# The recurrent mixer of a three-mixer network: its projections, its local part and its solve put in another order

## The chip, the cores and the metric

One core of one Trainium2 chip runs the whole program. The metric is device time in microseconds (us) of one execution; the kernel before took 1224.47 us, the median of three runs between 1223.39 and 1226.15. The engines are PE (TensorE, matrix products and their weight loads), DVE (VectorE), ACT (ScalarE), POOL (GpSimd) and SP (SyncE, which here only issues transfers). DRAM is the chip's large memory, SBUF the memory of the engines, PSUM the banks that PE writes.

## The reference

512 tokens of width 1024 pass two blocks (neighbourhood attention, then grouped attention, each followed by a gated projection) and then a hybrid layer, which is what this change is about. Cut to that layer:

```python
h = rms_norm_2(x, norm_g); proj = h @ w_in
(q, kc, vc, ks, vs, kw, vw, gl, g_nsa, rwkv_in, g_rwkv) = _split(proj, IN_SIZES)
o_nsa = nsa_mixer(...) * silu(g_nsa)             # compressed, selected and windowed attention
# the recurrent mixer, 8 heads of 64
prev = pad(p)[:, :-1]; p = p + shift_mu * (prev - p)          # p is rwkv_in
r, k, v, wd, ad = _split(p, (512, 512, 512, 64, 64))
w = w0 + tanh(wd) @ w_up; decay = exp(-exp(-softplus(-w) - 0.5)); a = sigmoid(a0 + ad @ a_up)
kk = normalised(k * k_k); k = k * (1 + (a - 1) * k_a)
for t:                                                         # per head
    state = state * w_t + (state @ -kk_t) (kk_t * a_t)^T + v_t k_t^T
    y_t = state @ r_t
y = group_norm(y) * gn_w + gn_b + sum(r * k * r_k) * v
return x + concat(o_nsa, y * silu(g_rwkv)) @ w_out
```

## The kernel before, in words

Weights come as a stream of 512 KB pieces: SP loads a piece (`wraw`), ACT rounds it to `whi` (L147) and DVE or POOL takes the difference `wlo` (L148; `N.lo` says which of the two). Each product is three matmuls, high with high, high with low and low with high. Activations are kept the same way, as `act` and `half` tiles.

The 512 tokens are four tiles of 128. The first two blocks hold them in a swapped order (token 64 r + c of an 8 x 64 grid stands at 8 c + r); the hybrid layer needs them in their natural order. A store to DRAM can put them back row by row, and `natural` (L330) copies the whole activation into natural order in SBUF.

The recurrent mixer turns the loop over tokens into chunks:

- **Projections.** `rwkv_proj` makes r, k and v for four heads (`hh` is 0 or 1), 96 matmuls of 256 columns for each. PE's result is copied by ACT (L796), multiplied by `shift_mu` on DVE (L797), subtracted on POOL (L798), and both pieces go to DRAM (`d_raw`), one of them a row later, so that a load brings a token and its predecessor. `rwkv_lowrank` makes decay and learning rate (`d_low`), with eight small float32 products (L769).
- **Local part.** `rwkv_local` runs eight times (two groups of heads, four token tiles). Each loads its `rkv` rows (L841) and `low` rows (L837), adds the two pieces (L844), normalises k (L853 to L857), forms decayed sums on PE (L865), transposes (L890), splits into high and low (`l_xl`, `l_tl`, L222), multiplies (L920), masks (`am`, `abq`, L925 and L926) and stores triangles (`d_a`) and other pieces. The pool has four `rkv` and two `low` buffers, so two of the eight are under way at a time.
- **Solve.** `rwkv_triangles` loads all triangles at once, 128 blocks of 32 x 32 (L951). `rwkv_solve` inverts them in 31 steps on DVE (L967, L969) and stores the inverses (`d_t`, L972), whose other entries were zeroed before (L736).
- **Chain.** `rwkv_applied` loads an inverse (L995) and multiplies (L1003, the first PE work that needs the solve), and the rest follows token tile by token tile.

Between these steps `products()` feeds PE with the sparse attention's keys and queries and with the gates of the recurrent mixer (`rwkv_gates`, four weight pieces). The code order is only a wish: a scheduler at build time interleaves what the code emits, and from then on each engine runs its own list strictly in order. SP's list and ACT's list hold the transfers too, so a transfer that waits holds up what stands behind it.

Of the kernel before, what the change touches and what calls it, by code (L numbers as in the profile page):

```python
# [123 lines left out]
class Net:  # L124
# [197 lines left out]
    def natural(self, act):  # L322

        out = self.new_act()
        nc = self.nc
        engines = iter(TT * (nc.vector.tensor_copy, nc.vector.tensor_copy, nc.scalar.copy, nc.scalar.copy))
        for t in range(TT):
            for a, o in zip(act, out):
                for ks in (slice(0, 4), slice(4, 8)):
                    next(engines)(o[:, ks].rearrange("p k (r c) -> p k r c", r=8)[:, :, :, 16 * t:16 * t + 16],  # L330
                                               a[:, ks, t * P:t * P + P].rearrange("p k (c r) -> p k r c", r=8))
        return out
# [391 lines left out]
    def rwkv_consts(self, pool):  # L724
# [7 lines left out]
        zero = pool.tile([P, 768], F32, name="rkv", bufs=4)  # L732
        nc.vector.memset(zero, 0.0)
        for t in range(TT):
            for h in range(2):
                nc.sync.dma_start(out=self.head_rows(self.d_t, t, 4 * h, 4), in_=zero[:, :512].rearrange("p (h n) -> p h n", h=4))  # L736
# [10 lines left out]
    def rwkv_lowrank(self, buf, act):  # L747

        nc = self.nc
        ps = self.cols(("r_wa",), act)  # L750
        raw, d = buf[:, 0], buf[:, 1]
        nc.scalar.copy(raw.rearrange("p (r t c) -> p t c r", r=8, t=TT), ps.rearrange("p (t c r) -> p t c r", t=TT, r=8))
# [3 lines left out]
        nc.vector.tensor_sub(d[:, 1:], raw[:, :S - 1], raw[:, 1:])  # L756
        nc.vector.tensor_scalar(d[:, 0:1], raw[:, 0:1], -1.0, None, op0=OP.mult)
        nc.vector.scalar_tensor_tensor(d, d, mu, raw, op0=OP.mult, op1=OP.add)

        for j, (up, row) in enumerate((("decay_up", "decay_w0"), ("iclr_up", "iclr_a0"))):  # L760
            l, m = buf[:, 2 + 2 * j], buf[:, 3 + 2 * j]
            nc.scalar.activation(l[0:64], d[64 * j:64 * j + 64], AF.Tanh if j == 0 else AF.Copy)
            nc.vector.memset(l[64:65], 1.0)
            nc.sync.dma_start(out=m[0:64], in_=self.a[up])
            nc.sync.dma_start(out=m[64:65], in_=bass.AP(tensor=self.a[row].tensor, offset=self.a[row].offset,
                                                        ap=[[S, 1], [1, S]]))
            for t in range(TT):
# [15 lines left out]
    def rwkv_proj(self, act, hh, names, mu, stage):  # L783

        nc = self.nc
        for name in names:
            n = "rkv".index(name)
            keys = [("r_" + name, hh, j) for j in range(2)]
            self.fetch(*keys)
            us = [self.w.pop(k) for k in keys]  # L790
            for tp in range(2):
                ps = self.group_rows(us, act, tp)
                r = stage(n, tp)
                p2 = ps.rearrange("p (t n) -> p t n", t=2)
                m = mu[:, names.index(name), None, :].to_broadcast([P, 2, 256])
                nc.scalar.copy(r[0], p2)  # L796
                nc.vector.tensor_tensor(r[1], p2, m, op=OP.mult)  # L797
                nc.gpsimd.tensor_tensor(r[0], r[0], r[1], op=OP.subtract)  # L798
                for t in range(2 * hh):
                    for d, a in zip(self.d_raw[hh], r):  # L800
                        o = bass.AP(tensor=d.tensor, offset=d.offset + (1 + 16 * (2 * tp + t)) * 768 + 256 * n, ap=[[768, 16], [64 * 768, 8], [1, 256]])
                        nc.sync.dma_start(out=o, in_=a[:, t])

    def rwkv_proj_first(self, act, mu):

        raw = [self.act_tile(self.act, j, F32).rearrange("p k n -> p (k n)") for j in range(2)]
        full = [a[:, :TT * 768].rearrange("p (t n) -> p t n", t=TT) for a in raw]
        self.rwkv_proj(act, 0, "rkv", mu, lambda n, tp: [a[:, 2 * tp:2 * tp + 2, 256 * n:256 * n + 256] for a in full])
        for t in range(TT):
            for d, a in zip(self.d_raw[0], full):  # L810
                o = bass.AP(tensor=d.tensor, offset=d.offset + (1 + 16 * t) * 768, ap=[[768, 16], [64 * 768, 8], [1, 768]])
                self.nc.sync.dma_start(out=o, in_=a[:, t])
        return [a[:, TT * 768:].rearrange("p (a t n) -> p a t n", a=2, t=2) for a in raw]

    def rwkv_params(self, pool, hh):
        par = {n: self.bcast(pool, n, 256 * hh, 256) for n in ("k_k", "k_a", "r_k")}
        return par
# [139 lines left out]
    def rwkv_solve(self, pool, A, T):  # L957

        nc = self.nc
        for s in range(31):  # L960
            for j0, j1 in ((0, min(s + 1, 8)), (8, s + 1)):
# [7 lines left out]
                nc.vector.tensor_tensor(tv, tv, o, op=OP.subtract)  # L969
        for t in range(TT):  # L970
# [767 lines left out]
```

## Time and profile before

| what | value |
|---|---|
| median of three runs | 1224.47 us |
| the profiled execution | 1225.36 us, span 1223.6 us, mean granted clock 0.969 |
| busy over the span | PE 1138.2 us (93%), DVE 851.1 (70%), ACT 623.0 (51%), POOL 395.8 (32%) |
| chain that ended last | PE 61%, DVE 17%, DMA 7%, ACT 5%, issue 5%, POOL 3% |
| projections, low rank and copies (721 to 793 us) | PE busy 64.24 of 72 us, clock 0.93 |
| seven of the eight locals (824 to 924 us) | PE busy 90.15, DVE 86.60 of 100 us, clock 0.91 |
| solve | 942.11 to 980.88 us; first matmul of the chain at 990.22 us |

The span runs from the first to the last instruction; the execution's own time is 1.8 us longer. A busy PE is not a PE at its peak: its matmuls overlap, so a stretch is judged by the time from one start to the next, by the waits and by the granted clock, which is 1 at 2.4 GHz and 0.5 at 1.2 GHz. Times on DVE, ACT and POOL can be added up, save for some 0.07 us by which neighbours overlap.

### The profile page before, as it was taken

How to read it: one execution, taken by the hardware profiler on the slowest of the kernel's cores; microseconds unless marked ns; L12 is line 12 of the kernel's file. 1: busy time of each engine (PE TensorE's matmuls, PEld its weight loads, DVE VectorE, ACT ScalarE, POOL GpSimd, SP SyncE). 2: the span in 40 equal slices, each digit the busy share in tenths (PEclk: the TensorE clock that was granted, in tenths of full speed). 3: DMA queues.
4: the chain of work that ended last, by engine and by line, in shares of the span. 5: the costliest groups of instructions: out<-in, count | busy, mean ns of one | idle time of the engine just before them, and what ended most of it. 6: DMA issues, size and time to landing. Idle time of an engine off the chain costs nothing.

```text
span 1223.6 us, 20514 instructions
## 1 busy us (share of the span) xinstructions
PE 1138.2 (93%) x7176; PEld 999.8 (82%) x7176; DVE 851.1 (70%) x2093; ACT 623.0 (51%) x1355; POOL 395.8 (32%) x549
## 2 busy tenths in 40 slices
PE   7999999998999989999999999799899799899896
PEld 5898989886889868877877898688789688798785
DVE  6566666657677877886676763489786925688865
ACT  5566565635443566566564642434444223267743
POOL 0021211110300364674311011164445523357731
PEclk9999999999999989999999999899799989899998
DMA  6333333213232310211132445774667553712511
GB/s 248 117 98 102 102 103 102 92 61 132 93 108 74 97 38 1 70 35 36 52 130 69 139 120 192 219 262 145 202 189 195 162 140 106 237 45 71 180 52 69
DMA packets 87040, 143.24 MB, mean 117 GB/s; under 512 B 21525, under 2 KB 52245, under 8 KB 86938
## 3 DMA queue, kind: packets, MB, share of 16 engines
q1 hardware_dynamic: 72344, 133.49, 34.3%
q10 hardware_dynamic: 14018, 6.36, 2.0%
q0 software_dynamic: 576, 2.10, 0.5%
q8 instruction: 56, 0.92, 0.3%
q14 instruction: 46, 0.38, 0.1%
HBM read 114.12 MB, written 27.79 MB: 116 GB/s over the span
## 4 chain that ended last, share of the span: by engine, by line
PE 61%; DVE 17%; DMA 7%; ACT 5%; issue 5%; POOL 3%; SPq 2%; ACTq 0%; POOLq 0%; DVEq 0%
PE mm L205 23%; PE mm L188 5%; PE mm L189 5%; PE mm L190 4%; PE sc L205 3%; PE mm L216 2%; DVE KT L967 2%; PE tr L492 1%; PE u L677 1%; PE tr L670 1%; DMA rkv<-d_raw 1%; PE ch L1003 1%; DVE big L969 1%; PE u L1373 1%; PE tr L318 1%
## 5 line engine op out<-in xcount | busy, mean ns | idle before, releaser
L205 PE MATMUL mm<-whi,act 128*128 128x256 f32 (+2 forms) x1344 | 356.2, 323 | 9.7 <-DVE x L347 3.5
L205 PE MATMUL mm<-wlo,act 128*128 128x256 f32 (+2 forms) x896 | 287.1, 321 | 0.5 <-POOL wlo L148 0.5
L205 PEld LDWEIGHTS mm<-whi,act 128*128 128x128 f32 x1344 | 239.8, 194 | 31.3 <-DVE x L347 5.5
L205 PEld LDWEIGHTS mm<-wlo,act 128*128 128x128 f32 x896 | 174.7, 195 | 10.3 <-POOL wlo L148 0.7
L147 ACT CAST whi<-wraw 128x1024 fp32r<-128x1024 f32 (+1 forms) x128 | 133.3, 1043 | 91.9 <-PE mm L205 38.5
L148 DVE TENSOR_TENSOR wlo<-wraw,whi 128x1024 fp32r<-128x1024 f32 x91 | 116.6, 1284 | 54.2 <-ACT whi L147 52.4
L205 PE MATMUL mm<-whi,half 128*128 128x256 f32 (+1 forms) x448 | 146.0, 327 | 4.2 <-DVE half L222 4.2
L148 POOL TENSOR_TENSOR wlo<-wraw,whi 128x1024 fp32r<-128x1024 f32 (+2 forms) x37 | 88.0, 2382 | 129.7 <-DVE rs_y L237 69.9
L188 PE MATMUL mm<-act,whi 128*128 128x512 f32 x312 | 126.1, 404 | 2.2 <-DVE b_qn L547 2.2
L190 PE MATMUL mm<-act,wlo 128*128 128x512 f32 x312 | 124.6, 399 | 0.0
L205 PEld LDWEIGHTS mm<-whi,half 128*128 128x128 f32 x448 | 88.4, 198 | 10.8 <-DVE half L222 5.1
L484 POOL TENSOR_SCALAR a_P<-a_P,a_rd 128x256 f32<-128x256 f32 x64 | 32.9, 517 | 156.5 <-DVE a_rd L483 143.9
L189 PE MATMUL mm<-half,whi 128*128 128x512 f32 x200 | 79.1, 396 | 0.0
L188 PEld LDWEIGHTS mm<-act,whi 128*128 128x128 f32 x312 | 59.9, 192 | 14.4 <-issue 3.4
L190 PEld LDWEIGHTS mm<-act,wlo 128*128 128x128 f32 x312 | 59.9, 192 | 12.2
L663 POOL TENSOR_SCALAR b_P<-b_P,b_rd 128x512 f32<-128x512 f32 x64 | 45.5, 715 | 54.6 <-DVE b_rd L662 44.0
L660 ACT ACTIVATE b_P<-sc,b_mn 128x512 f32<-128x512 f32 x64 | 44.1, 690 | 21.5 <-DVE b_mn L657 13.6
L657 DVE TENSOR_REDUCE b_mn<-sc 128x1 f32<-128x512 f32 x64 | 43.5, 684 | 10.6 <-PE sc L655 10.2
L478 DVE CUSTOM_DVE_ANT_0 a_P<-sc,a_bias 128x256 f32<-128x256 f32 x64 | 26.1, 421 | 34.7 <-PE tr L492 20.1
L1359 POOL TENSOR_SCALAR n_P<-n_P,b_rd,n_gl 128x128 f32<-128x128 f32 (+3 forms) x64 | 39.2, 619 | 30.6 <-DVE b_rd L1357 10.3
L222 DVE TENSOR_TENSOR b_pl<-tr,b_ph 128x512 fp32r<-128x512 f32 x64 | 43.3, 683 | 6.0 <-ACT b_ph L221 5.3
L189 PE MATMUL mm<-act,whi 128*128 128x512 f32 x112 | 45.8, 409 | 0.0
(396 smaller groups left out, 2826.8 us busy)
## 6 DMA issues: line engine op xcount, KB each, us to landing
wraw<-in_wstream SPq DMA_DIRECT2D x133, 512.0 KB, 3.6
a_bias<-in_bias SPq DMA_DIRECT2D x16, 384.0 KB, 3.1
rkv<-d_raw SPq DMA_DIRECT2D x16, 384.0 KB, 4.9
d_raw<-act SPq DMA_DIRECT2D x8, 384.0 KB, 5.6
xf<-x SPq DMA_DIRECT2D x4, 512.0 KB, 3.7
d_low<-low ACTq DMA_DIRECT2D x8, 256.0 KB, 2.8
d_t<-rkv SPq DMA_DIRECT2D x8, 256.0 KB, 4.2
low<-d_low SPq DMA_DIRECT2D x8, 256.0 KB, 3.3
```

The source lines that it names most:

```text
L147: nc.scalar.copy(hi[:, :m], raw[:, :m])
L148: self.lo.tensor_tensor(lo[:, :m], raw[:, :m], hi[:, :m].bitcast(F32), op=OP.subtract)
L188: nc.tensor.matmul(ps, lhsT=wh[:, kt], rhs=ah[:, kt], start=kt == 0, stop=False)
L189: nc.tensor.matmul(ps, lhsT=wh[:, kt], rhs=al[:, kt], start=False, stop=False)
L190: nc.tensor.matmul(ps, lhsT=wl[:, kt], rhs=ah[:, kt], start=False, stop=kt == KT - 1)
L205: nc.tensor.matmul(ps, lhsT=l, rhs=r, start=i == 0, stop=i == len(ops) - 1)
L222: (eng_lo or nc.vector.tensor_sub)(lo, src, hi.bitcast(F32))
L484: nc.gpsimd.tensor_scalar(w, w, rd, 0.5, op0=OP.mult, op1=OP.mult)
L657: nc.vector.tensor_reduce(mn, ps, axis=AX.X, op=OP.max, negate=True)
L660: nc.scalar.activation(pt, ps, AF.Exp, bias=mn, scale=1.0, accum_out=den)
L663: nc.gpsimd.tensor_scalar(pt, pt, rd, 0.5, op0=OP.mult, op1=OP.mult)
L1359: nc.gpsimd.tensor_scalar(w, w, rd, st["gl"][:, b, gc:gc + 1], op0=OP.mult, op1=OP.mult)
```

## The change

The first heads' r is projected from the swapped activation as the normalised tiles come in. The low rank follows (its products now take all 128 rows, with zeros and a row of ones put in by POOL beforehand), `natural` runs during it, in 16 copies of 512 elements by whole k tiles, and the first heads' k and v are projected from the natural activation, k and v of a token half one behind the other. Results go through ring buffers and are stored piece by piece; ACT's copy and POOL's subtraction are replaced by a subtraction on DVE that reads PSUM. The first four locals are emitted ahead of and between the other heads' r, k and v. The zeros of `d_t` are stored in the second block. The triangles are loaded in three pieces, the solve is emitted four steps at a time between `products()`, its result is stored by SP's queue, and the gates' `wlo` is made by DVE.

```diff
     def natural(self, act):
-        engines = iter(TT * (nc.vector.tensor_copy, nc.vector.tensor_copy, nc.scalar.copy, nc.scalar.copy))
-        for t in range(TT):
-            for a, o in zip(act, out):
-                for ks in (slice(0, 4), slice(4, 8)):
-                    next(engines)(o[:, ks]...[:, :, :, 16 * t:16 * t + 16], a[:, ks, t * P:t * P + P]...)
+        for k in range(KT):
+            for a, o, copy in zip(act, out, (nc.vector.tensor_copy, nc.scalar.copy)):
+                copy(o[:, k].rearrange("p (r c) -> p r c", r=8), a[:, k].rearrange("p (c r) -> p r c", r=8))
...
-        zero = pool.tile([P, 768], F32, name="rkv", bufs=4)
-        nc.vector.memset(zero, 0.0)
+    def zero_inverses(self, pool):
+        zero = pool.tile([P, 512], F32, name="zero", bufs=1)
+        nc.gpsimd.memset(zero, 0.0)
         for t in range(TT):
             for h in range(2):
                 nc.sync.dma_start(out=self.head_rows(self.d_t, t, 4 * h, 4), in_=...)
...
     def rwkv_lowrank(self, buf, act):
+        for j, (up, row) in enumerate((("decay_up", "decay_w0"), ("iclr_up", "iclr_a0"))):
+            nc.gpsimd.memset(m[64 - 64 * j:128 - 64 * j], 0.0)
...
+        for t in range(TT):
+            yield
+            for j in range(2):
                 ps = self.bank("sc")
-                nc.tensor.matmul(ps, lhsT=l[0:65, t * P:t * P + P], rhs=m[0:65], start=True, stop=True)
-                th = buf[:, 6 + t % 2]
+                nc.tensor.matmul(ps, lhsT=l[:, t * P:t * P + P], rhs=m, start=True, stop=True)
+                th = buf[:, (6, 7, 1)[(2 * t + j) % 3]]
...
-                nc.scalar.dma_start(out=self.d_low[j, t], in_=th)
+                nc.sync.dma_start(out=self.d_low[j, t], in_=th)
...
+    def rwkv_proj(self, act, hh, names, mu, stage, swapped=False):
+        for tp in range(2):
+            for name in names:
+                ps = self.group_rows(us[name], act, tp)
...
-                nc.scalar.copy(r[0], p2)
                 nc.vector.tensor_tensor(r[1], p2, m, op=OP.mult)
-                nc.gpsimd.tensor_tensor(r[0], r[0], r[1], op=OP.subtract)
-                for t in range(2 * hh):
+                nc.vector.tensor_tensor(r[0], p2, r[1], op=OP.subtract)
+                for t in range(2):
...
     def rwkv_triangles(self, pool):
-        nc.scalar.dma_start(out=A, in_=self.blocks(self.d_a))
+        for i, n in ((0, 96), (96, 16), (112, 16)):
+            nc.scalar.dma_start(out=A[i:i + n], in_=self.blocks(self.d_a, i, n))
...
     def rwkv_solve(self, pool, A, T):
+            yield
         for t in range(TT):
-            nc.scalar.dma_start(out=self.blocks(self.d_t, 32 * t, 32), in_=T[w])
+            nc.sync.dma_start(out=self.blocks(self.d_t, 32 * t, 32), in_=T[w])
...
                 if l == 1:
-                    rest = N.rwkv_proj_first(act, N.rwkv_mu(pool, 0, 0, 3, "mu0"))
-                    N.rwkv_lowrank(pool.tile([P, 8, S], F32, name="low", bufs=1), act)
-                    N.rwkv_proj(act, 1, "r", N.rwkv_mu(pool, 1, 0, 1, "mu1"), lambda n, tp: [a[:, tp] for a in rest])
+                    N.rwkv_proj(act, 0, "r", mu, ring, swapped=True)
+                    low = N.rwkv_lowrank(pool.tile([P, 8, S], F32, name="low", bufs=1), act)
+                    next(low)
+                    act = N.natural(act)
+                    for _ in low:
+                        pass
+                    N.rwkv_proj(act, 0, "kv", mu, ring)
...
-                N.rwkv_proj(act, 1, "kv", N.rwkv_mu(loc, 1, 1, 3, "mu"), stage)
-                act = N.natural(act)
-                N.lo = nc.gpsimd
                 for hh in range(2):
-                    par = N.rwkv_params(loc, hh)
+                    if hh:
+                        par = N.rwkv_params(loc, hh)
+                        N.lo = nc.gpsimd
                     for t in range(TT):
                         N.rwkv_local(loc, hh, t, par, st)
+                        if hh == 0 and t < 3:
+                            N.rwkv_proj(act, 1, "rkv"[t], mu, stage)
...
-            N.rwkv_solve(chn, *sv)
+            solve = N.rwkv_solve(chn, *sv)
...
+                N.lo = nc.vector
                 for _ in N.rwkv_gates(pool, act):
                     yield
+                N.lo = nc.gpsimd
...
             for n, _ in enumerate(products()):
+                for _ in range(4 if n < 9 else 0):
+                    next(solve, None)
```

SP's list around the first local's loads, before (L736 zeroes `d_t`, L686 loads `k_k`, `k_a` and `r_k`, L802 stores the other heads' projections, L837 and L841 are the loads of a local):

```order
L780 DMA mu<-in_shift_mu 128x2x256
L686 DMA k_k<-in_k_k 128x256
L736 DMA d_t<-rkv 128x4x128 x8
L686 DMA k_a<-in_k_a 128x256
L686 DMA r_k<-in_r_k 128x256
L837 DMA low<-d_low 128x2x256
L802 DMA d_raw_84<-st_8768 16x8x256 x2
L802 DMA d_raw_83<-st_8767 16x8x256 x2
L841 DMA rkv<-d_raw_81 128x768
```

And now (L812 stores projections: `d_raw_81` and `_82` are the first heads', `_83` and `_84` the other heads'; L841 and L845 are the loads):

```order
L812 DMA d_raw_82<-pu 128x256 x2
L812 DMA d_raw_81<-th 128x256 x2
L789 DMA mu<-in_shift_mu 128x3x256
L683 DMA r_k<-in_r_k 128x256
L683 DMA k_k<-in_k_k 128x256
L683 DMA k_a<-in_k_a 128x256
L725 DMA rkv<-in_tri 128x384
L725 DMA rkv<-in_ind 128x2
L841 DMA low<-d_low 128x2x256
L845 DMA rkv<-d_raw_81 128x768
L845 DMA rkv<-d_raw_82 128x768
L812 DMA d_raw_84<-st_8851 128x256 x2
```

The eight stores of zeros are gone from here. The last stores of the first heads' v stand ahead of the loads of the first local, and the stores of the other heads' r (`d_raw_84`), which stood ahead of them, behind.

POOL's list at the first local, before (L798 subtracts in a projection, L847 and L848 belong to the first local, L148 makes a `wlo`):

```order
L798 TENSOR_TENSOR st_8767<-st_8767,st_8768 128x512
L148 TENSOR_TENSOR wlo<-wraw,whi 128x1024
L798 TENSOR_TENSOR st_8825<-st_8825,st_8826 128x512
L847 TENSOR_TENSOR rt<-rkv,k_k 128x256
L848 TENSOR_TENSOR rt<-low,k_a 128x256
L798 TENSOR_TENSOR st_8895<-st_8895,st_8896 128x512
L148 TENSOR_TENSOR wlo<-wraw,whi 128x1024 x2
L798 TENSOR_TENSOR st_8953<-st_8953,st_8954 128x512
L148 TENSOR_TENSOR wlo<-wraw,whi 128x1024
```

And now (L851, L852 belong to a local, as do L943 to L949):

```order
L413 MEMSET n_Klw_10957 64x512 x2
L851 TENSOR_TENSOR rt<-rkv,k_k 128x256
L852 TENSOR_TENSOR rt<-low,k_a 128x256
L943 TENSOR_TENSOR rt<-rkv,rt 128x256
L948 TENSOR_TENSOR rt<-rkv 128x256
L949 TENSOR_TENSOR rt<-rt,r_k 128x256
L851 TENSOR_TENSOR rt<-rkv,k_k 128x256
L852 TENSOR_TENSOR rt<-low,k_a 128x256
L943 TENSOR_TENSOR rt<-rkv,rt 128x256
L944 TENSOR_TENSOR rt<-low,rt 128x256
```

No subtraction and no `wlo` stands among POOL's work for the first locals any more.

DVE's list at the end of the solve, before (L967 and L969 are the solve, L1233 takes the low part of transposed queries, on which PE waits for a bank):

```order
L969 TENSOR_TENSOR big_10239<-big_10239,KT 128x20x4
L1233 TENSOR_TENSOR half_11179<-mm,half_11179 64x2x256
L967 TENSOR_TENSOR KT<-big_10239,big_10237 128x24
L967 TENSOR_TENSOR KT<-big_10239,big_10237 128x63
L1233 TENSOR_TENSOR half_11179<-mm,half_11179 64x2x256
L969 TENSOR_TENSOR big_10239<-big_10239,KT 128x8x3
```

And now (L974 is the solve, L1239 the queries' low part):

```order
L974 TENSOR_TENSOR big_10263<-big_10263,KT 128x22x2
L972 TENSOR_TENSOR KT<-big_10263,big_10259 128x8
L972 TENSOR_TENSOR KT<-big_10263,big_10259 128x23
L974 TENSOR_TENSOR big_10263<-big_10263,KT 128x8
L974 TENSOR_TENSOR big_10263<-big_10263,KT 128x23
L1239 TENSOR_TENSOR half_11203<-mm,half_11203 64x2x256 x4
```

The four low parts that stood between the last steps of the solve now follow it.

## Rows read from the trace of the kernel before

**Rows 1.** Windows. Columns: stretch, length, busy us (instructions) by engine, granted clock, DMA share, GB/s.

```profile
721.00:793.00 72.00, 64.24 (x446) 58.52 (x444) 30.38 (x41) 28.66 (x36) 13.47 (x14) 0.93 0.60 187
793.00:824.00 31.00, 28.64 (x168) 25.89 (x169) 24.57 (x39) 10.94 (x24) 20.20 (x15) 0.88 0.83 273
824.00:924.00 100.00, 90.15 (x713) 82.44 (x713) 86.60 (x240) 47.17 (x162) 45.71 (x56) 0.91 0.57 175
924.00:991.00 67.00, 56.16 (x403) 51.83 (x404) 47.23 (x134) 19.82 (x35) 31.55 (x32) 0.92 0.69 179
991.00:1224.00 233.00, 211.10 (x1500) 188.73 (x1498) 154.59 (x463) 112.17 (x268) 102.15 (x139) 0.96 0.34 109
```

**Rows 2.** Chain that ended last: start us, us, what.

```profile
720.84 22.66 PE mm L205 x189
...
754.61 1.72 PE sc L769 x4
...
934.42 7.59 DMA big<-d_a
...
983.79 6.38 DMA big<-d_t
...
1165.56 2.76 PE mm L216 x12
```

**Rows 3.** Timeline of SP's queue: start us, us, line, transfer, count.

```profile
780.91 6.09 SPq L736 DMA_DIRECT2D d_t<-rkv  x8
...
789.80 2.50 SPq L802 DMA_DIRECT2D d_raw<-st  x4
792.34 1.08 SPq L841 DMA_DIRECT2D rkv<-d_raw  x2
```

**Rows 4.** The tile d_raw: time from issue to landing of its transfers.

```profile
DMA to landing us min/median/max: 2.3/4.2/7.5
```

**Rows 5.** Timeline of DVE, projections and first local: start, us, line, shapes, idle time before.

```profile
763.65 1.23 DVE L148 TENSOR_TENSOR wlo<-wraw,whi 128x1024 fp32r<-128x1024 f32 x1 [1.62 <-ACT whi L147]
...
772.66 4.59 DVE L330 CAST act<-act 128x512 fp32r<-128x512 f32 x8 [1.85 <-DMA d_raw<-act]
...
799.15 0.96 DVE L844 TENSOR_TENSOR rkv<-rkv 128x768 f32<-128x768 f32 x1 [4.38 <-DMA rkv<-d_raw]
...
805.14 2.32 DVE L236 TENSOR_SCALAR l_i<-l_ss 128x4 int32<-128x4 int32 x1
...
813.50 2.04 DVE L844 TENSOR_TENSOR rkv<-rkv 128x768 f32<-128x768 f32 x1
...
823.80 0.69 DVE L222 TENSOR_TENSOR l_tl<-x,l_th 128x512 fp32r<-128x512 f32 x1
```

**Rows 6.** Groups of ACT, 760 to 785 us: busy us, mean ns of one.

```profile
L330 ACT CAST act<-half 128x512 fp32r<-128x512 f32 x8 | 8.6, 1176 | 0.1
```

**Rows 7.** Timeline of POOL, the same stretch.

```profile
805.04 4.75 POOL L148 TENSOR_TENSOR wlo<-wraw,whi 128x1024 fp32r<-128x1024 f32 x2
```

**Rows 8.** Timeline of DVE, last local and solve.

```profile
923.86 0.69 DVE L222 TENSOR_TENSOR l_tl<-x,l_th 128x512 fp32r<-128x512 f32 x1 [0.60 <-ACT l_th L221]
...
942.11 0.19 DVE L967 TENSOR_TENSOR KT<-big,big 128x31 f32<-128x31 f32 x1 [4.54 <-DMA big<-d_a]
...
942.82 1.79 DVE L969 TENSOR_TENSOR big<-big,KT 128x31 f32<-128x31 f32 x1
...
952.88 2.68 DVE L967 TENSOR_TENSOR KT<-big,big 128x152 f32<-128x152 f32 x2
...
976.22 0.68 DVE L1233 TENSOR_TENSOR half<-mm,half 64x512 fp32r<-64x512 f32 x1
...
980.56 0.32 DVE L969 TENSOR_TENSOR big<-big,KT 128x8 f32<-128x8 f32 x2
```

**Rows 9.** Timeline of ACT behind the solve.

```profile
980.90 2.71 ACTq L972 DMA_DIRECT2D d_t<-big  x4
```

**Rows 10.** PE's waits, 680 to 1000 us: total us, times, longest us.

```profile
PE mm L1229 <- DVE half L1233: 8.4, 1, 8.4
```

More of the change, by code (lines that the diff above doesn't have):

```diff
@@ L755, in rwkv_lowrank @@
                                               ap=[[1, P], [1, 1]]))
-        nc.vector.tensor_sub(d[:, 1:], raw[:, :S - 1], raw[:, 1:])
-        nc.vector.tensor_scalar(d[:, 0:1], raw[:, 0:1], -1.0, None, op0=OP.mult)
-        nc.vector.scalar_tensor_tensor(d, d, mu, raw, op0=OP.mult, op1=OP.add)
+        rest = self.small.tile([P, 1], F32, name="wa_rest", bufs=1)
+        nc.vector.tensor_scalar(rest, mu, -1.0, 1.0, op0=OP.mult, op1=OP.add)
+        ms = []
         for j, (up, row) in enumerate((("decay_up", "decay_w0"), ("iclr_up", "iclr_a0"))):
[L761 to L767, printed above, removed]
+            m, one = buf[:, 3 + 2 * j], 64 - 64 * j
+            nc.gpsimd.memset(m[64 - 64 * j:128 - 64 * j], 0.0)
+            nc.sync.dma_start(out=m[64 * j:64 * j + 64], in_=self.a[up])
+            nc.sync.dma_start(out=m[one:one + 1], in_=bass.AP(tensor=self.a[row].tensor, offset=self.a[row].offset, ap=[[S, 1], [1, S]]))
+            l = buf[:, 2 + 2 * j]
+            nc.gpsimd.memset(l[64 - 64 * j:128 - 64 * j], 0.0)
+            nc.gpsimd.memset(l[one:one + 1], 1.0)
@@ new lines, in rwkv_lowrank @@
+        ps = self.cols(("r_wa",), act)
+        raw, d = buf[:, 1], buf[:, 0]
+        nc.scalar.copy(raw.rearrange("p (r t c) -> p t c r", r=8, t=TT), ps.rearrange("p (t c r) -> p t c r", t=TT, r=8))
+        nc.scalar.mul(d, raw, rest)
+        nc.vector.scalar_tensor_tensor(d[:, 1:], raw[:, :S - 1], mu, d[:, 1:], op0=OP.mult, op1=OP.add)
+        for j in range(2):
+            w = slice(64 * j, 64 * j + 64)
+            nc.scalar.activation(buf[w, 2 + 2 * j], d[w], AF.Tanh if j == 0 else AF.Copy)
@@ L781, in rwkv_mu @@
         return mu
-    def rwkv_proj(self, act, hh, names, mu, stage):
+    def rwkv_proj(self, act, hh, names, mu, stage, swapped=False):
         nc = self.nc
[L786 to L792, printed above, removed]
+        keys = {name: [("r_" + name, hh, j) for j in range(2)] for name in names}
+        self.fetch(*sum(keys.values(), []))
+        us = {name: [self.w.pop(k) for k in keys[name]] for name in names}
+        for tp in range(2):
+            for name in names:
+                n = "rkv".index(name)
+                ps = self.group_rows(us[name], act, tp)
@@ L802, in rwkv_proj @@
                         nc.sync.dma_start(out=o, in_=a[:, t])
[L804 to L813, printed above, removed]
@@ L815, in rwkv_params @@
-    def rwkv_params(self, pool, hh):
-        par = {n: self.bcast(pool, n, 256 * hh, 256) for n in ("k_k", "k_a", "r_k")}
+    def rwkv_params(self, pool, hh):
+        par = {}
+        for n in ("r_k", "am", "k_k", "k_a"):
+            if n != "am":
+                par[n] = self.bcast(pool, n, 256 * hh, 256)
+            elif hh == 0:
+                pool.tile([P, 256], F32, name="am", bufs=2)
         return par
@@ L1531, in tile_net, with ring @@
                 if l == 1:
-                    rest = N.rwkv_proj_first(act, N.rwkv_mu(pool, 0, 0, 3, "mu0"))
-                    N.rwkv_lowrank(pool.tile([P, 8, S], F32, name="low", bufs=1), act)
-                    N.rwkv_proj(act, 1, "r", N.rwkv_mu(pool, 1, 0, 1, "mu1"), lambda n, tp: [a[:, tp] for a in rest])
+                    mu = N.rwkv_mu(pool, 0, 0, 3, "mu0")
+                    names = iter(TT * (("pp", 4), ("pp", 4), ("th", 2), ("pu", 2)))
+                    def ring(n, tp):
+                        two = [next(names) for _ in range(2)]
+                        return [pool.tile([P, 512], F32, name=k, bufs=b).rearrange("p (t n) -> p t n", t=2) for k, b in two]
+                    N.rwkv_proj(act, 0, "r", mu, ring, swapped=True)
[5 more added lines that the diff above has]
+                    N.rwkv_proj(act, 0, "kv", mu, ring)
         if stop == "xf":
```

22 lines of the change are left out of this document (13 added, 9 removed).

## The prediction, written before the result was known

> **What bounds the kernel now.** I read the windows first, because one share for the whole span hides the stages. From 721 to 991 us PE is busy 239.2 of 270 us, so 30.8 us of it are idle; the granted clock there is 0.93, 0.88, 0.91 and 0.92, and one minus the clock times each length (5.0, 3.7, 9.0 and 5.4) makes 23.1 us lost to it. Behind 991 us PE is busy 211 of 233 us at 0.96 [rows 1]. So this change has some 54 us in reach if PE's work stays the same; the reader is to see that PE is nearly full and that a large gain needs fuller PE earlier, not less waiting of others. The chain of waits shows where the path leaves PE: matmuls from 720.84 on, low rank at 754.61, then the triangles' load at 934.42 and the inverses' load at 983.79 [rows 2], with the solve between them, 942.11 to 980.88 [rows 8]. DVE has 86.6 of 100 us in the local part, so it is nearly as full as PE there [rows 1].
>
> **The sum, part by part.** Taken against the profiled execution (1225.36 us, span 1223.6), which is 0.9 us over the median of 1224.47.
>
> *Start of the first local, -27.3.* Its first operation stands at 799.15 [rows 5]. Before it, in the old order, came the other heads' r, k, v, the copies, the eight zero stores (6.09 us of SP) and four projection stores (2.50) [rows 3]. In the new order the last columns of r remain when the last swapped tile is there; the 189 matmuls begin at 720.84 behind its transposes [rows 2], and I allow a microsecond for its copies, so about 722. By the new list some 24 matmuls of r remain, which at 0.12 us (22.66 / 189) are 2.9 and fall mostly into that microsecond and the next; the product for the low rank 24 at 0.23 (2.76 / 12) is 5.5, so about 729 to 730. The copies run beside it, eight of 4.59 us in all on DVE [rows 5] and eight of 8.6 on ACT [rows 6], to about 731. Then k and v, 192 at 0.12, are 23.0, and eight low rank products at 0.43 (1.72 / 4) are 3.5: 757.5. Two operations on PSUM follow, where the nearest row is an operation of the same shape with one PSUM input, 0.69 [rows 5]: 1.4. Four stores issue in 2.5 [rows 3], a store lands after 4.2 in the middle [rows 4], and from the load's issue to the first addition pass 6.8 (792.34 to 799.15 [rows 3, 5]): 771.9. Bounds: 769 with landings of 2.3 and the copies wholly hidden; 784 if the copies come only behind the low rank's chain (8.6) and landings take 7.5 (3.3). So -30 to -15.
>
> *First local, 0.* It takes 24.65 us to its last split (799.15 to 823.80). POOL's two `wlo` hold 4.75 us in it [rows 7], and beside them DVE's operations on 128 x 4 numbers, two of which take 2.32 each where one on 128 x 31 takes 0.19 [rows 5, 8], and an addition takes 2.04 instead of 0.96: 5.3 us over. These POOL operations are gone, but DVE gets three `wlo` (1.23 each [rows 5]) and three subtractions (0.69), 5.8. Bounds -7 (DVE waits anyway) and +5.8.
>
> *The seven other locals, +10.* They take 100.06 us now (823.80 to 923.86 [rows 5, 8]), 14.3 from one to the next. The new lists put 676 PE instructions where 542 stood, since the other heads' projections fall between the locals: 134 at 0.12 are 16.1. PE has 9.85 us idle there; if these all fill, 6.3 remain; DVE gains 2.5 (two subtractions and two mults of 0.69, some moved out). Bounds: +2.5, if DVE alone paces, and +18.6, if both add. I take 10, nearer to PE, as PE's busy time is the larger.
>
> *Triangles' load, -1.* One load of 7.59 [rows 2] becomes three, and only the last, an eighth of it, waits for the last local. The path from issue to use was 6.8 for the much smaller `rkv` load, so the fixed part rules. Bounds -4.3 and 0.
>
> *Solve, -3.1.* Four low parts of 0.68 go behind it (-2.8), one `wlo` comes in (+1.2), and one of POOL's holds goes (1.79 where the last steps take 0.16: -1.5) [rows 8]. Bounds 0, and -12 if the holds by the other `wlo` go too (for instance 2.68 for a pair where 0.4 is usual, four times).
>
> *Inverses, +2.* Four stores take 2.71 on ACT now [rows 9] and 2.50 on SP [rows 3]: nothing. But the load of the inverse stays in ACT's list, waits there for the landing, and ACT's copies of queries stand behind it; PE already waited 8.4 us for a low part of the same queries [rows 10]. Bounds 0 and +4.
>
> The row on these stores is the 2.71 and 2.50 us of issue [rows 3, 9]. The Trainium skill (Trainium Kernel Development and Optimization, Key Constraints) says that the queues of SP, ACT and POOL run on the same DMA engines, so that another issuer saves sequencer time alone. By it the transfer gains nothing and only ACT's 2.7 us come free; were the landing faster by SP, the path would lose some of the 6.38 us behind it. I go by the rows.
>
> *Behind the first product of the chain, +3.2.* 14 matmuls of 512 columns at 0.23 that were done before it now follow. Bounds 0 (they fill idle time) and 3.2.
>
> The zeros stored in the second block I cost at nothing: what stands behind them on SP there are weight loads, which run ahead of their use. If that cover is gone, it is SP's 6.09 us.
>
> Sum: -27.3 + 0 + 10 - 1 - 3.1 + 2 + 3.2 = -16.2. Span 1207.4, execution 1209.2, and with the 0.9 off 1208.3: **1208 us**. All bounds together run from -50.6 to +16.6 (1174 to 1241); the lower end is also what PE's 54 us in reach allow.
>
> **Rivals.**
>
> *B, PE paces the local part.* PE's idle share of 9.85 in 100 comes back whatever its work, because a local's PE steps wait for DVE in turn; 16.1 / 0.9015 = 17.9 are added instead of 10. For it: 90.15 us busy, clock 0.91 [rows 1]. Against: the added matmuls wait for nothing from DVE, so they fit in gaps. 1216 us.
>
> *C, DVE's stretched operations are the local part's limit.* With POOL emptied of `wlo` up to the second group of heads, DVE is held less, the cadence grows only by 2.5 and the solve loses four more holds of some 2.3 us: -7.5 - 9 = 1192 us. For it: 2.32 instead of 0.19 [rows 5]. Against: the second group of locals still has POOL's `wlo`.
>
> POOL's hold is seen only in DVE operations such as those at 805.14 and 813.50, while the split at 823.80 takes its 0.69 [rows 5, 7]. The Trainium skill (SBUF — State Buffer, Who interferes with whom) says that the port pair of the two engines is locked for a whole instruction, and that a VectorE operation with at most one SBUF input outside the two-port modes does not contend. By it the subtraction that now reads PSUM is never held, while the gates' `wlo`, with two SBUF inputs, can be held by POOL and hold it in turn, which speaks against moving them; the trace agrees with the first as far as the split shows it, and by the second the solve's gain of 3.1 would be 1.5 or so less.
>
> *D, slower: SP's queue holds the locals up.* The loads of the second to fourth local stand in one list with the other heads' 24 stores, and each store waits for its projection, 96 matmuls of 0.12 or 11.5 us of PE. If each of three locals waits for one projection, 34.6 come on top: 1243 us. It decides from the point where the first four locals follow each other at over 14.3 + 16.2 / 3 = 19.7 us instead of 14.3. For it: the first local's load waited 4.38 us now [rows 5]. Against: four `rkv` buffers let loads run ahead by up to four locals, and PE does the projections in the same order.
>
> *E, PE's work is only shifted.* What PE gains ahead of the solve it idles away behind it, because the 211 busy of the last 233 us hang on something else than the solve. The end then moves by the filled idle time of the projections alone, between nothing and 7.8 us (72 less 64.24): 1217 to 1225. For it speaks little: the chain does pass through the solve and the inverses' load [rows 2, 8].
>
> **Chances.** The sum 0.42, B 0.25, C 0.17, D 0.08, E 0.08. A difference under 0.2% (2.4 us) can't be told from none. Faster: the sum, C and nearly all of B, with 0.03 of E, 0.86. No change: 0.05, from E and the edge of B. Slower: D and a bit of B, 0.09. The range, 1188 to 1222, takes in the sum with most of its bounds, B and all but the far end of C; outside are D and half of E.
>
> **What would show it.** Right: the first addition of a local at about 772, the first low split at 796 and the last at 906, the solve from about 923 to 959, the first product of the chain at some 971 to 972 us, and PE idle by about 15 us instead of 30.8 between 721 and there. B shows as a last split near 914. C as a distance of 14.6 us between locals with no DVE operation stretched, and a solve under 30 us. D as locals that wait for `rkv` loads queued behind stores. It is wrong if the first addition stands later than 784, if PE's idle time reappears in front of the first product, or if the end does not move with that product.

## The result and the profile after

The changed kernel took 1210.12 us, the median of four runs, against 1225.31 for the kernel before: a ratio of 0.9883 (95% interval 0.9866 to 0.9901). Measured again beside the experiments it took 1212.72 against 1225.85 (0.9857, 0.9812 to 0.9903). The forecast was 1208. Its profiled execution is the longest of those four, 1214.51 us with a span of 1212.7, so steps are read from it and from the profile of the repeat (span 1213.2) together.

The page's first section of the kernel after, busy us with the share of the span:

```profile
PE 1135.9 (94%) x7176; PEld 997.9 (82%) x7176; DVE 844.1 (70%) x2105; ACT 619.0 (51%) x1344; POOL 376.5 (31%) x540
```

PE does the same 7176 matmuls. Its idle time over the span is 1212.7 - 1135.9 = 76.8 us, where it was 85.4. The stretches of [rows 1], now:

```profile
721.00:793.00 72.00, 69.87 (x512) 63.66 (x512) 42.08 (x82) 32.54 (x47) 12.61 (x16) 1.00 0.68 220
793.00:824.00 31.00, 28.21 (x206) 24.00 (x205) 25.79 (x65) 12.32 (x38) 16.49 (x15) 1.00 0.67 210
824.00:924.00 100.00, 88.86 (x699) 82.96 (x698) 75.88 (x195) 42.27 (x139) 35.18 (x47) 0.92 0.55 166
924.00:991.00 67.00, 60.88 (x448) 58.37 (x448) 42.73 (x132) 21.56 (x33) 27.43 (x33) 0.94 0.69 191
```

From 721 to 824 us PE now works 98.1 of 103 us (92.9 before) and its granted clock is 1.00 instead of 0.93 and 0.88, so it gets through 718 matmuls where it did 614. In the next 100 us it is about as full as before. Lines of DVE's timeline that answer to [rows 5] and [rows 8]:

```profile
769.18 0.69 DVE L805 TENSOR_TENSOR st<-mm,mu 128x512 f32<-128x512 f32 x1 [5.34 <-DMA mu<-in_shift_mu]
...
775.80 0.96 DVE L848 TENSOR_TENSOR rkv<-rkv 128x768 f32<-128x768 f32 x1 [1.18 <-DMA rkv<-d_raw]
...
799.26 0.68 DVE L222 TENSOR_TENSOR l_tl<-x,l_th 128x512 fp32r<-128x512 f32 x1
...
911.17 0.69 DVE L222 TENSOR_TENSOR l_tl<-x,l_th 128x512 fp32r<-128x512 f32 x1 [0.82 <-ACT l_th L221]
...
919.25 0.41 DVE L930 TENSOR_TENSOR abq<-x,tri 128x256 f32<-128x256 f32 x1
...
933.86 0.19 DVE L972 TENSOR_TENSOR KT<-big,big 128x31 f32<-128x31 f32 x1 [0.47 <-DMA big<-d_a]
...
937.27 1.22 DVE L148 TENSOR_TENSOR wlo<-wraw,whi 128x1024 fp32r<-128x1024 f32 x1
...
954.51 4.78 DVE L974 TENSOR_TENSOR big<-big,KT 128x88 f32<-128x88 f32 x2
...
965.34 0.32 DVE L974 TENSOR_TENSOR big<-big,KT 128x8 f32<-128x8 f32 x2
```

The first addition, both splits, the last mask, the first and the last step of the solve are the marks of the sum. The last mask and the chain's first product before, which [rows 8] does not hold, and that product now:

```profile
929.78 0.41 DVE L926 TENSOR_TENSOR abq<-x,tri 128x256 f32<-128x256 f32 x1
990.22 1.16 PE L1003 MATMUL ch<-act,big 128*128 128x128 f32 x8 [1.67 <-DMA big<-d_t]
```

```profile
977.22 1.05 PE L1009 MATMUL ch<-act,big 128*128 128x128 f32 x8
```

One hold by POOL is left in the solve (4.78 us for a pair). PE's waits from 918 to 1000 us, in the same form as [rows 10], of the kernel after and then of its repeat:

```profile
PE mm L205 <- POOL wlo L148: 5.9, 1, 5.9
PE mm L1156 <- POOL st L1128: 2.4, 1, 2.4
PE mm L1235 <- ACT st L1257: 0.3, 1, 0.3
```

```profile
PE mm L205 <- POOL wlo L148: 3.9, 1, 3.9
PE mm L1235 <- DVE half L1239: 3.2, 1, 3.2
PE mm L1156 <- POOL st L1128: 2.4, 1, 2.4
```

The 8.4 us behind the solve are gone or 3.2, and a wait for a low part made by POOL has come in their place.

### The profile page after: what moved, and what is told of

Read it like the earlier page. It is cut to its first block, busy times and chain, and to the rows that moved or that the text cites. A ratio compares the mean times of both kernels' runs of the same rounds, so it can differ in the third digit from the quotient of the medians.

```text
span 1212.7 us, 20550 instructions
## 1 busy us (share of the span) xinstructions
PE 1135.9 (94%) x7176; PEld 997.9 (82%) x7176; DVE 844.1 (70%) x2105; ACT 619.0 (51%) x1344; POOL 376.5 (31%) x540
## 5 line engine op out<-in xcount | busy, mean ns | idle before, releaser
L205 PE MATMUL mm<-whi,act 128*128 128x256 f32 (+2 forms) x1504 | 373.1, 321 | 6.5 <-ACT act L221 2.9
L205 PEld LDWEIGHTS mm<-whi,act 128*128 128x128 f32 x1504 | 259.4, 194 | 30.4 <-ACT act L221 5.2
L148 DVE TENSOR_TENSOR wlo<-wraw,whi 128x1024 fp32r<-128x1024 f32 x95 | 118.8, 1254 | 56.8 <-ACT whi L147 55.1
L188 PE MATMUL mm<-act,whi 128*128 128x512 f32 x312 | 124.4, 399 | 2.7 <-DVE b_qn L544 2.7
L148 POOL TENSOR_TENSOR wlo<-wraw,whi 128x1024 fp32r<-128x1024 f32 (+2 forms) x33 | 77.7, 2359 | 98.3 <-DVE rs_y L237 70.0
L205 PE MATMUL mm<-whi,half 128*128 128x256 f32 (+1 forms) x288 | 98.1, 341 | 3.9 <-DVE half L222 3.5
L205 PEld LDWEIGHTS mm<-whi,half 128*128 128x128 f32 x288 | 55.4, 193 | 10.1 <-DVE half L222 5.3
L657 ACT ACTIVATE b_P<-sc,b_mn 128x512 f32<-128x512 f32 x64 | 44.1, 690 | 21.5 <-DVE b_mn L654 13.6
L654 DVE TENSOR_REDUCE b_mn<-sc 128x1 f32<-128x512 f32 x64 | 43.5, 684 | 10.9 <-PE sc L652 10.4
L1361 ACT ACTIVATE n_P<-n_P,b_mn 128x128 f32<-128x128 f32 (+3 forms) x64 | 35.8, 561 | 21.0 <-DVE b_mn L1358 12.8
```

The source lines that it names most:

```text
L148: self.lo.tensor_tensor(lo[:, :m], raw[:, :m], hi[:, :m].bitcast(F32), op=OP.subtract)
L188: nc.tensor.matmul(ps, lhsT=wh[:, kt], rhs=ah[:, kt], start=kt == 0, stop=False)
L205: nc.tensor.matmul(ps, lhsT=l, rhs=r, start=i == 0, stop=i == len(ops) - 1)
L654: nc.vector.tensor_reduce(mn, ps, axis=AX.X, op=OP.max, negate=True)
L657: nc.scalar.activation(pt, ps, AF.Exp, bias=mn, scale=1.0, accum_out=den)
```

## The experiments

The PE theory: PE's list sets the time. Its work is fixed, so the time is that work plus PE's idle time plus what the granted clock takes, and the moment of the chain's first product counts only where PE runs out of other work. The path theory, on which the prediction's sum stands: the steps along the path add up to the end. Each expectation says what its own A and B are. Each kernel was timed 6 to 12 times. "Clock" is the mean over a kernel's timed runs, "idle" the span less PE's busy time in its one profile, "split" and "first product" the last low split of the locals and the first product of the chain in that profile.

| kernel | median us | ratio to before (95%) | clock | idle | split | first product |
|---|---|---|---|---|---|---|
| before (58 runs) | 1225.3 to 1225.9 | 1 | 0.970 | 85.4 | 923.9 | 990.2 |
| after, again | 1212.7 | 0.9857 (0.9812, 0.9903) | 0.977 | 78.5 | 911.9 | 981.4 |
| e1 other heads ahead | 1223.7 | 0.9980 (0.9954, 1.0006) | 0.972 | 83.2 | 911.4 | 982.7 |
| e2 gates' low parts by POOL | 1220.8 | 0.9951 (0.9927, 0.9975) | 0.970 | 82.8 | 911.3 | 974.1 |
| e12 both undone | 1218.6 | 0.9935 (0.9913, 0.9957) | 0.973 | 76.2 | 911.2 | 972.5 |
| e7 k and v swapped | 1213.2 | 0.9892 (0.9850, 0.9934) | 0.978 | 76.7 | 912.5 | 980.7 |
| b1 gates alone, in before | 1225.9 | 0.9994 (0.9973, 1.0014) | 0.971 | 87.9 | 930.0 | 1003.8 |
| e5 solve at once | 1212.1 | 0.9887 (0.9856, 0.9919) | 0.977 | 73.1 | 908.1 | 973.0 |
| e6 subtraction on POOL | 1215.9 | 0.9917 (0.9885, 0.9949) | 0.973 | 79.1 | 910.8 | 978.4 |
| e9 all low parts on VectorE | 1216.7 | 0.9922 (0.9894, 0.9949) | 0.978 | 81.4 | 908.5 | 984.2 |
| e3 inverses by ACT | 1214.4 | 0.9899 (0.9867, 0.9931) | 0.977 | 76.6 | 911.2 | 980.4 |
| e4 one load of triangles | 1212.9 | 0.9899 (0.9864, 0.9935) | 0.976 | 72.2 | 907.1 | 979.3 |
| e10 two more low parts on VectorE | 1213.1 | 0.9888 (0.9858, 0.9919) | 0.976 | 77.4 | 909.3 | 983.2 |

**The changed kernel again.** No edit.

> The changed kernel once more, so that the others have it on the same chip. Both theories: 1209 to 1212 us. Its profile tells which marks are steady: first addition of a local 776, first and last low split 799 and 911, solve 934 to 966, first product of the chain 977 us (all within 1.5 us); if the single profile seen so far was a late one (it took 1214.5 us), what is lost lies behind 911 us.

The time, 1212.7, is just over the expected 1209 to 1212. The marks stand up to the start of the solve (first addition 775.3, splits 799.4 and 911.9, solve 935.1), but the solve ends at 971.7 instead of 965.7 and the first product comes 4.2 us later. The spans still differ by 0.5 us only. From the first product to the end, in the first profile and in the repeat:

```profile
977.22:1212.70 235.48, 216.40 (x1519) 192.30 (x1517) 154.92 (x464) 113.38 (x270) 105.10 (x140) 0.95 0.34 110
```

```profile
981.43:1213.20 231.77, 211.30 (x1519) 187.41 (x1517) 154.13 (x464) 113.44 (x271) 106.45 (x140) 0.98 0.36 115
```

The same 1519 matmuls stand behind the product, and the repeat does them at a granted clock of 0.98 instead of 0.95. So this pair does not show that a late product is free. The guess that the first profile lost its time behind 911 us is not borne out.

**The other heads ahead of the locals.**

```diff
+                for n in "rkv":
+                    N.rwkv_proj(act, 1, n, mu, stage)
                 for hh in range(2):
...
-                        if hh == 0 and t < 3:
-                            N.rwkv_proj(act, 1, "rkv"[t], mu, stage)
```

> The other heads' r, k, v stand ahead of the first local again, everything else stays. Theory A (the gain is the place of these projections: they fill PE's idle time among the locals): first addition later by about three projections of 11.5 us, so at 800 to 810 us; the seven locals return from 112 to about 100 us; solve 15 to 23 us later, and the time 1222 to 1233 us. Theory B (the gain comes from the new way of projecting, ring buffers, natural copies by whole tiles and from POOL being freed): most of the gain stays, 1208 to 1216 us.

The time is as A gave it (1223.7), the marks are not: the first addition did not move to 800 but stood at 771.9, the first split at 805.3, and the last at 911.4, 0.5 us from where it was in the repeat. PE has done 1400 matmuls from 721 to its last mask, against 1403 in the kernel after: the same work by about the same time, in another order. The loss comes behind. PE's waits from 918 to 1000 us:

```profile
PE mm L1235 <- DVE half L1239: 8.8, 1, 8.8
PE ch L1009 <- DMA big<-d_t: 3.1, 1, 3.1
PE mm L205 <- POOL wlo L148: 0.6, 1, 0.6
```

PE is through with what it may do and waits for a low part of queries, as it did before [rows 10]. DVE's timeline shows where that stands, between the last steps of the solve:

```profile
970.16 0.69 DVE L1239 TENSOR_TENSOR half<-mm,half 64x512 fp32r<-64x512 f32 x1
970.89 0.34 DVE L974 TENSOR_TENSOR big<-big,KT 128x32 f32<-128x32 f32 x2
971.26 0.69 DVE L1239 TENSOR_TENSOR half<-mm,half 64x512 fp32r<-64x512 f32 x1
971.99 1.94 DVE L972 TENSOR_TENSOR KT<-big,big 128x24 f32<-128x24 f32 x2
```

**The gates' low parts by POOL.**

```diff
-                N.lo = nc.vector
+                N.lo = nc.gpsimd
                 for _ in N.rwkv_gates(pool, act):
```

> The low parts of the gates' weights are made by POOL again. Theory A (POOL's operations hold DVE while the solve runs): the solve takes 35 to 39 us instead of 31.8, the first product of the chain comes 3 to 7 us later, time +2 to +6 us over the changed kernel. Theory B (PE's matmuls ahead of the chain hide the solve): solve longer, the time within 2 us.

8 us longer, more than A or B had. The solve takes 34.2 us and the first product comes at 974.1, earlier than in both profiles of the kernel after, so the product's moment does not show the loss. PE's idle time does: from 721 us to that product it is 27.2 us, 22.2 in the kernel after, and 1564 matmuls are left behind it, not 1519. PE's waits in the same stretch show a part of the loss:

```profile
PE mm L1156 <- POOL st L1128: 5.7, 1, 5.7
PE mm L205 <- DVE st L404: 3.9, 1, 3.9
PE ch L1009 <- DMA big<-d_t: 2.8, 1, 2.8
```

The matmuls of L1156 need what POOL makes in L1123 to L1128, and two `wlo` of 4.69 us in all, begun at 917.90, stand ahead of it in POOL's list. In the kernel after this wait is 2.4 us, so 3.3 of the 8 us stand here. The mean clock is lower too (0.970 beside 0.977), and the rest is not traced to one wait.

**The first heads' k and v swapped too.**

```diff
-                    N.rwkv_proj(act, 0, "r", mu, ring, swapped=True)
+                    N.rwkv_proj(act, 0, "rkv", mu, ring, swapped=True)
...
-                    N.rwkv_proj(act, 0, "kv", mu, ring)
```

> The first heads' k and v are projected from the swapped activation too, together with r, ahead of the low rank. Theory A (natural copies are hidden, PE is full there): first addition within 3 us of 776, time within 2 us of the changed kernel. Theory B (the natural order is what lets loads start, by plain stores of whole rows and later ones): first addition 4 to 8 us later and the time 3 to 6 us longer.

The first addition came at 784.4, 8.6 us late, just over B's 4 to 8; no longer time can be told (1213.2 beside 1212.7, intervals overlapping and some 5 us wide to either side). The windows of this kernel:

```profile
721.00:775.00 54.00, 45.78 (x261) 37.02 (x259) 23.10 (x37) 22.78 (x28) 0.25 (x2) 0.87 0.50 155
775.00:845.00 70.00, 63.36 (x479) 57.62 (x477) 59.05 (x132) 23.98 (x64) 33.55 (x32) 1.00 0.73 234
845.00:912.00 67.00, 65.72 (x541) 61.45 (x542) 57.47 (x155) 31.57 (x110) 25.50 (x33) 0.95 0.61 177
```

Here PE is idle for 8.2 us up to 775 us and the granted clock there is 0.87, where the kernel after has 2.1 us idle (51.87 busy of the same 54) and 1.00. Then it is fuller from 845 to 912 us (65.72 against 60.09 busy), and the last split is back at 912.5, the first product at 980.7. So this run tests the first addition alone: its 8.6 us were made up before the end of the locals.

**The gates alone, in the kernel before.** One part of the change put into the old kernel:

```diff
+                N.lo = nc.vector
                 for _ in N.rwkv_gates(pool, act):
                     yield
+                N.lo = nc.gpsimd
```

> The kernel before with one part of the change alone: VectorE makes the gates' low parts. Theory A (time is PE's idle time; there PE waited 0.5 us for a low part of POOL and 8.4 us for a query's low part behind the solve on DVE): the solve's 38.8 us shorten by 2 to 5, but the time stays within 2 us of the kernel before. Theory B (taking these four operations off POOL is a gain by itself, as undoing it cost 8 us): 1217 to 1221 us.

No gain (A). And more: the solve took 41.9 us, not less, and the first product came 13.6 us later:

```profile
1003.82 1.16 PE L1003 MATMUL ch<-act,big 128*128 128x128 f32 x8 [0.95 <-DMA big<-d_t]
```

Yet the time is the same, and behind that product pass 215.2 us instead of 233.4: the scheduler had put other work ahead of it. PE's share of it, from 721 us to the first product, before and in b1 (columns as in [rows 1]):

```profile
721.00:990.22 269.22, 238.40 (x1721) 217.90 (x1719) 188.77 (x452) 106.59 (x255) 110.15 (x116) 0.92 0.64 190
```

```profile
721.00:1003.82 282.82, 248.83 (x1848) 229.82 (x1846) 192.99 (x459) 111.60 (x263) 106.89 (x117) 0.95 0.63 186
```

In b1 127 more matmuls stand ahead of the product, and so fewer behind it (1399 instead of 1504). With e2 (product at 974.1, 1220.8 us) this is the plainest evidence that the moment of the first product alone does not set the end.

**The solve emitted at once.**

```diff
-                for _ in range(4 if n < 9 else 0):
+                for _ in range(40 if n == 0 else 0):
```

> All steps of the solve are emitted in one go ahead of the keys' products, as before, the rest stays. Theory A (the steps' order on DVE is nearly the same either way): within 2 us of the changed kernel. Theory B (the fine emission is what keeps the queries' low parts behind the solve and PE supplied): 3 to 8 us longer, with a wait of PE for a low part of queries of 8 us back.

A: no difference (1212.1), and no wait of 8 us.

**ACT's copy and POOL's subtraction back.**

```diff
+                nc.scalar.copy(r[0], p2)
                 nc.vector.tensor_tensor(r[1], p2, m, op=OP.mult)
-                nc.vector.tensor_tensor(r[0], p2, r[1], op=OP.subtract)
+                nc.gpsimd.tensor_tensor(r[0], r[0], r[1], op=OP.subtract)
```

> In the projections ACT copies the result and POOL subtracts again, instead of VectorE's subtraction from PSUM. Theory A (PE paces up to the last local, DVE has room): the last low split stays at 911 within 2 us, time within 2 us of the changed kernel. Theory B (POOL's subtractions hold DVE in the local part): last split 4 to 8 us later and the time 3 to 6 us longer.

The last split stays (910.8), against B; the time is 3 us longer with an interval that overlaps that of the repeat, so it can't be told from none.

**All low parts on VectorE.**

```diff
-                N.lo = nc.gpsimd
                 for _ in N.nsa_rows(keep, pool, act, st, ns):
```

> VectorE makes the low parts of the sparse attention's query and gate weights as well, all that POOL still made between the last local and the next stage. Theory A (PE's waits of 3.9 to 5.9 us for a low part of POOL around 951 us are real): they go, the solve lengthens by two to four operations of 1.23 us, time 2 to 5 us under the changed kernel. Theory B (DVE is the fuller engine there, and the solve's length is what counts): time 2 to 5 us longer.

POOL's wait goes as A said, but the solve grows to 41.3 us, DVE becomes what PE waits for, and the time is 4 us longer (with overlapping intervals). B is nearer.

**The inverses by ACT.**

```diff
-            nc.sync.dma_start(out=self.blocks(self.d_t, 32 * t, 32), in_=T[w])
+            nc.scalar.dma_start(out=self.blocks(self.d_t, 32 * t, 32), in_=T[w])
```

> The inverses are stored from ACT's queue again, the rest of the change stays. Theory A (the time is PE's idle time plus what the granted clock takes; the moment of the chain's first product does not set the end): the first product may come 1 to 3 us later, the time within 2 us of the changed kernel. Theory B (the path runs through these stores): as many us longer as the product comes later, 2 to 4.

No difference that can be told (A): the product at 980.4, the time 1214.4.

**One load of triangles.**

```diff
-        for i, n in ((0, 96), (96, 16), (112, 16)):
+        for i, n in ((0, 128),):
```

> The triangles are loaded by one transfer again. Theory A: the start of the solve moves by 2 us or less either way (14.2 us passed from the last mask to it with three loads, 11.9 with one), time within 2 us of the changed kernel. Theory B (ACT's 6.7 us for issuing three loads hold its copies up and so PE): 2 to 4 us faster.

No difference either (A). The three loads cost ACT this, in the kernel after:

```profile
924.01 5.01 ACTq L956 DMA_DIRECT2D big<-d_a  x2
...
929.06 1.67 ACTq L956 DMA_DIRECT2D big<-d_a  x1
```

and one load this:

```profile
919.89 0.40 ACTq L956 DMA_DIRECT2D big<-d_a  x1
```

Three loads held ACT's list for 6.7 us instead of 0.4. Yet the time can't be told from that of the repeat.

**Both undone.** The edits of e1 and e2 in one kernel:

```diff
+                for n in "rkv":
+                    N.rwkv_proj(act, 1, n, mu, stage)
...
-                        if hh == 0 and t < 3:
-                            N.rwkv_proj(act, 1, "rkv"[t], mu, stage)
...
-                N.lo = nc.vector
+                N.lo = nc.gpsimd
```

> The other heads' projections ahead of the locals and the gates' low parts on POOL, both undone together; undone one at a time they cost about 11 and 8 us. Theory A (both keep PE supplied in the same place, under triangles and solve, so that either loss is most of the whole): 1221 to 1227 us, the level of the kernel before. Theory B (two separate gains): 1229 to 1232 us.

Neither theory: 1218.6, less than with either one undone. With the other heads ahead, giving the gates to POOL is a gain of 5 us (1223.7 to 1218.6; the intervals just touch); in the kernel after it is a loss of 8; in the kernel before it makes no difference. So the 11 and the 8 us are not prices that the two edits carry with them. That they come from the lists which the scheduler makes of each mixture is the likely reason, and no run tests it by itself.

**Two more low parts on VectorE**, an attempt to beat the changed kernel: the gates' and the first two query pieces.

```diff
-                N.lo = nc.gpsimd
                 for _ in N.nsa_rows(keep, pool, act, st, ns):
+                    N.lo = nc.gpsimd
                     yield
```

> VectorE makes the low parts of the first two query weight pieces as well, POOL again all behind them. Theory A (PE's wait of 3.9 to 5.9 us for such a low part, which stands in POOL's list behind a multiplication that waits for a load, is what is still to be had, and all pieces on VectorE were too many): the wait goes, time 2 to 4 us under the changed kernel. Theory B (VectorE's solve gets longer and PE waits for the queries behind it): same or up to 3 us longer.

The same time, against A. POOL's wait was exchanged for one of 6.7 us for the queries' low part, behind a solve of 41.4 us.

## Why the prediction came out

The direction and the range held. The time was forecast 2 us too low by the first median and 5 us by the repeat. That it was only 2 is partly luck: against the two profiles, on which the steps can be read, the sum is over 5 us too low, as errors of up to 5 us in single steps partly cancel. The steps, in us, against the marks of the two profiles of the kernel after:

| step | forecast | after | again |
|---|---|---|---|
| first addition | -27.3 | -23.4 | -23.9 |
| first local | 0 | -1.2 | -0.6 |
| seven locals | +10 | +11.9 | +12.5 |
| last split to last mask | not in the sum | +2.2 | +2.1 |
| mask to solve | -1 | +2.3 | +2.9 |
| solve | -3.1 | -7.0 | -2.2 |
| solve to first product | +2 | +2.2 | +0.4 |
| behind that product | +3.2 | +2.1 | -1.6 |
| sum | -16.2 | -10.9 | -10.4 |

**Start.** Sized about right. The prediction's own terms add up to 772.4, not 771.9, so the forecast is -26.8 by them. PE was done with k and v at 762, not 757.5, though busy 40.5 of the 41 us from 721: it had 270 matmul records there, the sum 248. Six small loads then stood between the last stores and the first local's loads on SP. The list under "The change" has them, the sum has not:

```profile
764.99 0.44 SPq L789 DMA_DIRECT2D mu<-in_shift_mu  x1
...
766.99 0.43 SPq L725 DMA_DIRECT2D rkv<-in_tri  x1
...
768.42 1.01 SPq L845 DMA_DIRECT2D rkv<-d_raw  x2
```

**Locals.** Right in size, and not for the sum's reason. The sum took 134 more matmuls from the lists and let more than half of PE's 9.85 us of idle time fill with them. The stretch from the first split to the last, before and after:

```profile
823.80:923.86 100.06, 90.23 (x715) 82.52 (x713) 86.66 (x239) 47.24 (x162) 45.57 (x56) 0.91 0.57 176
```

```profile
799.26:911.17 111.91, 102.05 (x778) 93.31 (x778) 88.77 (x233) 46.58 (x153) 41.66 (x48) 0.94 0.57 177
```

Only 63 more matmuls stand there, and nothing was filled: PE is idle for 9.8 us before and 9.9 us after, and the stretch is longer by PE's added busy time (11.8 us). Most of that idle time is a wait for the masks that DVE makes, as rival B had it (busy us and mean ns, then idle us and what ended it, in the same two stretches):

```profile
L928 PE MATMUL x<-rkv,am 128*128 128x64 f32 x56 | 11.9, 297 | 7.6 <-DVE abq L926 7.5
```

```profile
L932 PE MATMUL x<-rkv,am 128*128 128x64 f32 x56 | 11.9, 298 | 8.7 <-DVE abq L930 8.7
```

B's 17.9 us are too dear because it priced all 134. C (2.5) is too cheap, and D did not come: the first four splits follow each other at 13.8, 20.2 and 15.1 us, and only the second distance is over D's 19.7.

**POOL's hold.** The prediction took the split at 823.80 to show that an operation which reads PSUM is not held by POOL. POOL stood idle then, so that split shows nothing. The one at 923.86 [rows 8] does, once: it took 0.69 us too, beside a `wlo` of POOL. POOL's timeline before, around the first split and the last:

```profile
821.58 0.74 POOL L945 TENSOR_TENSOR rt<-rt,r_k 128x256 f32<-128x256 f32 x1
826.15 0.73 POOL L939 TENSOR_TENSOR rt<-rkv,rt 128x256 f32<-128x256 f32 x1 [3.83 <-ACT GC L886]
...
922.34 2.37 POOL L148 TENSOR_TENSOR wlo<-wraw,whi 128x1024 fp32r<-128x1024 f32 x1
```

**Solve and triangles.** Both wrong in size, and what they are worth is not shown: the solve took 31.8 us in one profile of the same kernel and 36.5 in the next, with spans 0.5 us apart but different clocks behind the product.

**Where the reasoning falls short** is the step from the path to the end. For the change itself it held: the first product came 13.0 us earlier, 15 more matmuls stand behind it (14 were forecast), and the span is 10.9 us shorter. But the prediction opened with PE's 54 us in reach and then summed marks along one path, taking it that the end moves with the chain's first product. By itself that product does not tell the end: across the kernels it lies between 972.5 and 1003.8 us, and the time behind it between 215 and 249 us, longer where more matmuls are left (1399 in b1, 1504 before, 1519 after, 1564 in e2). Its moment tells something only together with the work left behind it and the clock there. Where 1519 or 1520 matmuls are left (after, again, e4, e5, e6), products from 973.0 to 981.4 go with spans from 1208.8 to 1213.2, so a late product does not look free there. A first addition 8.6 us late (e7) had been made up by the last split. And one sign of the prediction missed. From 721 us to the product PE was to be idle by some 15 us instead of 30.8, and it was idle by 22.2 us, in the repeat by 23.9:

```profile
721.00:977.22 256.22, 234.03 (x1749) 215.67 (x1749) 182.97 (x464) 103.08 (x245) 86.33 (x100) 0.95 0.64 195
```

The sum's largest terms, an earlier start and locals that cost PE's price, are also statements about PE's work from 721 us to the last split. That this is why it came close is argued and not tested.

What agrees with the time is the prediction's first paragraph. PE's idle time fell from 85.4 to 76.8 and 78.5 us, and across the fourteen profiles the span goes with it (correlation 0.85). As a span is PE's busy and idle time by definition, this says where the time went and not why. Most of the rest goes with the granted clock: within the kernels' 159 timed executions, 0.01 more of mean clock goes with 6.5 us less span, and the mean went from 0.970 to 0.977, some 4.5 of the 15 us. Set to one clock of 0.975 by that slope, spans are 1221 to 1222 before, 1210 to 1211 after, 1219 in e1, 1216 in e2, and 1215 in e12 and e7. That the clock is a cause is not shown: no run changed it alone, and across the profiles idle time and mean clock hardly go together (correlation -0.22).

**Still open.** Which part brings the gain. The place of the other heads' projections and the gates' engine matter most in the present lists, but not as a sum, and with both undone 7 of the 13 us are still there. No run took the early r, the low rank of 128 rows or the early zeros away. Nor can one profile of each kernel carry the idle times to a microsecond: e12's was taken on an execution of 1212.55 us, one of its two shortest, where the median is 1218.6.

## What to carry to other kernels

Where one engine is busy 93% with fixed work, forecast its idle time and its clock stretch by stretch; here the moment of the chain's first product did not tell the end without the work left behind it. Count the work that a stretch really holds, and see what its idle time waits for, before letting added work fill it: the locals' 9.8 us stayed. Undo parts in pairs before giving one of them a price: in a kernel whose order is made by a scheduler, moving the gates' low parts from POOL to DVE took 8 us off the time, changed nothing, and added 5 us (the last with intervals that just touch) in three surroundings. When work leaves a queue, look at what else stood behind it there: in e2, 3.3 of the 8 us stand as PE's wait for POOL's small operations behind two `wlo`, and none of it as a later first product.

## What was not expected of the hardware

Issuing three loads of the blocks (96, 16 and 16 partitions, rows of 32 numbers) took ACT's queue 5.01 us for two and 1.67 for the third, against 0.40 for one load of all 128. In e5's profile the three stand singly, at 0.35, 4.61 and 0.50 us: the first cost as little as the single load, and it was the second, behind it, that held the list. The solve began 14.2 us behind the last mask with three loads, 15.9 with one in e4 and 11.9 with one in the kernel before.
